# Scores of two attention branches: the keys' low parts in both halves of the partitions, and a second product over all 128 rows

## The chip, the cores and the metric

The kernel runs on one core of one Trainium2 chip. The metric is the device time of one launch in microseconds (us), the median of three runs. A difference below about 0.2% of it cannot be told from no change for this kernel: its three runs lie between 1477.23 and 1478.5 us.

## The reference, cut to what matters

Two layers of a hybrid block work on 256 latent tokens and 256 context tokens of width 1024. Each layer normalizes the tokens, projects them, and runs three attention branches side by side: grouped-query attention (8 query heads that share 2 key heads, 64 features a head), neighbourhood attention (8 heads of 64 features, with a bias for each position in the window), and latent attention (8 heads of 96 features). The branches are gated and merged, and a squared-ReLU MLP follows. The part that the change touches is the score of a query against a key, in the first two branches:

```
sc = jnp.einsum('bqkgd,btkd->bkgqt', qblk, k).astype(jnp.float32) * scale
p = jax.nn.softmax(sc, axis=-1).astype(v.dtype)
```

The context's queries are needed in the first layer alone, so there a head has two blocks of 128 latent queries against 512 keys and two blocks of 128 context queries against 256 keys; in the second layer it has the two latent blocks alone.

## The kernel before, in words

**Products.** TensorE (PE) takes float32r operands, which carry fewer bits than float32. So every operand is split in a high part (rounded) and a low part (what is left), and a product is made of three: high by high, high by low, low by high. The helper `mm3` (lines 762 to 764) issues these three for nearly all of the kernel. ScalarE (ACT) makes the high parts, VectorE (DVE) the low parts; for weights these are lines 699 and 700, one pair of instructions for a tile of 128x1024.

**Scores.** A head of 64 features fills only half of the 128 partitions that PE sums over. The neighbourhood and grouped-query branches use this: `stack_q` puts a head's high query parts on its own 64 partitions and its low parts on the other 64, and `stack_k` puts the head's high key parts in both halves. So one product over 128 rows (line 1518) makes high by high and low by high at once. A second product (line 1519) adds query-high by key-low. It reads only the head's own 64 partitions (rows 0 to 63 or 64 to 127), because there the key's low parts lie, in half of a slot. The latent branch has 96 features and uses `mm3` over 96 rows.

**One attention job** is a block of 128 queries of one head: scores on PE, the row's maximum on DVE (line 1654, or 1641 to 1645 with the bias), the exponential on ACT (1661), the scaling by the reciprocal sum on DVE (1672) or ACT (1670), four transposes on PE (1690 or 1694), the split of the transposed probabilities on ACT and DVE (808, 809). When the jobs of a head are done, PE multiplies with the values (1724, 1725). Three buffers hold the jobs under way. The branches run in the order neighbourhood, latent, grouped-query.

**What sets the order.** Every piece of work is a thread that asks for engines, buffers and events. A planner with a rough clock (fixed costs for each instruction, 0.43 us for a pair of score products) decides at build time which waiting instruction is issued next on each engine; on the chip each engine then runs its list in that order. Attention comes first where it can run, and dense items (projections, gates, output products) fill the rest. The dense items stand in a list (`SEQ`): `q k v` with a number are the neighbourhood branch's projections, `a0 a1 a2` those of the grouped-query branch, `g` gates. Of the grouped-query items, `a0` and `a1` wait until `a2` has got its slots (`gaslots`).

**Memory.** Everything but the weights lives in 41 slots of 4 KB a partition, which are lent in the order of the dense items (`needs`); a HALF or HALF_R is half a slot, a WHOLE a slot. Split weights have three tile pairs of their own (`wh0`, `wh1`, `wh2` with `wl0` to `wl2`); parts of the list add pairs out of slots for a while, but where the second layer's attention begins there are just the three. A weight tile takes a free pair as soon as it has arrived, and gives it back after its product.

Of the kernel before, what the change touches and what calls it, by code (L numbers as in the profile page):

```python
# [10 lines left out]
F32 = mybir.dt.float32  # L11
# [20 lines left out]
# attention units (pairs of heads) run in this order of branches, and so do their projections  # L32
# [11 lines left out]
# offsets in the packed column constants  # L44
# [8 lines left out]
RAW = 3          # weight tiles as they come from DRAM  # L53
SPLIT = 3        # weight tiles split in two parts
SLOTS = 41       # 4 KB slots (a partition) for everything else


# ---------------------------------------------------------------------------
# The schedule: the dense items in order, with the weight tiles that each one
# reads; shared by the host's packing and the program.  Words:  # L60
#   c0-7 first scale and shift by chunks; w 128 features of a later part of the modulation;
#   crow: room for the conditioning vectors as rows, until drop;
#   q k v + number: neighbourhood attention's projections; ckv rope l0-3: latent attention's;
#   a2 a0 a1 at: grouped-query attention's; yN yL yG: room for a branch's attention output
#   sN ...: that output split; gN0-7 oN0-3 ...: a branch's gates and products; W: output projection; M: MLP
# ---------------------------------------------------------------------------
# [16 lines left out]
def mix(items, extra, every=1):  # L83
    """`extra` spread among `items`, one after every `every` of those that read weights."""
    out, n, extra = [], 0, list(extra)
    for i in items:
        out.append(i)
        if i[2]:
            n += 1
            if extra and n % every == 0:  # L90
                out.append(extra.pop(0))
    assert not extra, len(extra)
    return out


def halves_of(l):
    """The token ranges that the sums before a norm are made in, latents first."""
    return [0, 1] if l == 0 else [0]


def word(l, w, wms):
    """The items of one word of SEQ."""
# [62 lines left out]
MLP_W = 48       # chunks of the modulation taken beside the first layer's MLP  # L165
# [92 lines left out]
WINDOW = (12, 8, 17)     # at the start, beside attention, otherwise  # L258
# [11 lines left out]
# ---------------------------------------------------------------------------  # L270
# The order of the instructions.  Every piece of the work is a thread (a
# generator) that asks for engines, buffers and events.  A rough clock of the
# engines decides which of the waiting instructions is issued next.
# ---------------------------------------------------------------------------
# [10 lines left out]
class Lender:  # L285
    """Lends a set of things; the lowest order is served first."""
# [24 lines left out]
class Arena(Lender):  # L311
    """Slots of [P, 2, T] words: WHOLE is a float32r slot (WHOLE_F float32), HALF and HALF_R are
    halves of a float32 or float32r one."""
# [43 lines left out]
class Banks(Lender):  # L357
    """PSUM banks, with a limit for each kind of use."""
# [19 lines left out]
class Window(Lender):  # L378
    """How many items may be under way."""
# [14 lines left out]
class Planner:  # L394
# [78 lines left out]
    def post(self, th, cmd):  # L473
        """Queues an instruction; ("any", ((engine, cost, fn), ...), slack) goes to the first that is free."""
# [10 lines left out]
    def dispatch(self):  # L485
        for e, p in self.pend.items():
            p[:] = [w for w in p if not w[4]]
            if p and self.busy[e] <= self.now + 1e-9:
# [4 lines left out]
                # TensorE runs at half its clock until it has been busy for a while  # L493
# [16 lines left out]
def a_(n):  # L510
    """Rough time of a ScalarE instruction over n columns."""
    return 0.07 + n * 0.00085
# [6 lines left out]
def v2_(n):  # L519
    return 0.07 + n * 0.00065  # L520


class Leaf:
    """Buffers that are given back after the last of n uses."""
# [10 lines left out]
class Opnd:  # L535
    """A (hi, lo) operand and the events that it waits for."""
# [8 lines left out]
class Prog:  # L545
# [22 lines left out]
    def fork(self, gen, pri=None):  # L568
        """A thread of its own, at the order of the item that is being built."""
        self.spawn(gen, self.cur[0], self.cur[1] if pri is None else pri)  # L570
# [39 lines left out]
    def needs(self, name, args):  # L610
        """The slots that an item owns; they are lent in the order of the items."""
# [4 lines left out]
        if name == "nak":  # L616
            return [WHOLE, HALF_R]
# [10 lines left out]
        if name == "gatr":  # L628
            return [pair] * 4 + [WHOLE, HALF_R]
# [30 lines left out]
    def take(self, mem, kind=WHOLE):  # L660
        """One of an item's own slots."""
# [5 lines left out]
    def take_pair(self, mem, n):  # L667
        """A slot for a (hi, lo) pair of n columns."""
# [15 lines left out]
    def transfer(self, n):  # L684
        """A transfer of n columns from when its descriptors are out."""
# [20 lines left out]
    def weights(self, keys, uses=1):  # L706
        """The split tiles of an item, given back after `uses` items have read them."""
# [15 lines left out]
    def it_raw(self, n, mem):  # L723
        """n more buffers for weights from DRAM, until it_less."""
# [15 lines left out]
    def it_more(self, n, mem):  # L740
        """n more buffers for split weights, until it_less."""
# [24 lines left out]
    def acc(self, out, a, b):  # L766
        """out = sum over k of a[k]^T b[k]; operands are (hi, lo) or Opnd."""
# [18 lines left out]
    def wcols(tl, n, w, c0=0, cw=None, off=0):  # L786
        """[(hi, lo)] of n row chunks in a split tile of row width w, columns c0:c0+cw."""
# [3 lines left out]
    def hcols(self, h, j):  # L791
        """h with features on partitions; j: 0 latents, 1 context, None both, by events of their own."""
# [11 lines left out]
    def hilo(self, hi, lo, src, n, scale=None, slack=0.0):  # L804
        """hi = round(src*scale), lo = src*scale - hi (both float32r)."""
# [15 lines left out]
    def it_wmc(self, l, c, mem):  # L821
        """Chunk c of the first scale and shift: both are wanted before anything else can start."""
# [37 lines left out]
    def it_crow(self, mem):  # L860
        """The two conditioning vectors along the columns of every partition, until it_drop."""
# [28 lines left out]
    def it_wm(self, l, part, fc, mem):  # L890
        """128 features of one of the modulation's six parts, as dot products along the columns."""
# [5 lines left out]
        # in the last layer the context is only normalized  # L897
# [33 lines left out]
    def stat(self, st, c, x, n, pos):  # L931
        """Adds the squares of chunk c to the sums of range st; the last chunk stays by itself."""
# [21 lines left out]
    def rstd(self, st, n, pos):  # L954
        """1/rms with tokens on partitions, one column for each 128 tokens."""
        nc = self.nc
        # the table of Sqrt is brought in before it is waited for
# [20 lines left out]
    def rstd_rows(self, st, n, pos):  # L978
        """1/rms of every token, on every partition (a PSUM bank)."""
# [14 lines left out]
    def norm_buffers(self, mem, key):  # L994
        """Sums of squares and three temporaries."""
# [33 lines left out]
    def norm_half(self, l, sc, sh, h, j):  # L1029
# [25 lines left out]
        if sc == SC1 and j == 1:  # L1055
            # the context's last use
# [4 lines left out]
    def it_start(self, mem):  # L1061
# [6 lines left out]
        # the conditioning vectors padded to 32 columns, and room for products of theirs  # L1068
# [62 lines left out]
    def project(self, keys, n, after):  # L1131
        """One weight tile, n tokens; `after(bank)` takes the product from its bank."""
# [1033 lines left out]
```

## Time and profile before

| | |
|---|---|
| median of three runs | 1477.95 us |
| lowest, highest | 1477.23, 1478.5 us |
| span of the profiled execution | 1471.1 us |
| busy share of the span: PE, DVE, ACT | 98%, 73%, 51% |
| chain that ended last: share of PE | 97% |
| score products: line 1518, line 1519 | 96, 96 |

The profiled execution is one run of its own; its span counts from the first to the last instruction. The median of the runs lies 6.85 us above it. In the profile, a group's row gives line, engine, operation, the tiles written and read, their shapes and count, then busy time and the mean ns of one, then the idle time of the engine before them. A matmul's duration there includes the time to run through the array, so the cost of one in a stream is read from start to start in the timeline. PEld is the load of the weights (the stationary operand), which can overlap a running matmul.

### The profile page before, as it was taken

What the parts mean: (1) busy time and instruction counts of PE and PEld (TensorE: products, weight loads), DVE (VectorE), ACT (ScalarE), POOL (GpSimd) and SP (SyncE); (2) the same over time, 40 slices, a digit from 0 to 9 for tenths busy, and PEclk for the clock granted to TensorE, in tenths of its full rate; (3) what the DMA queues carried; (4) which work ended last, traced back from release to release, by engine and by line L of the source; (5) the groups of instructions that cost most, each with busy time, mean ns of one, the idle gap of its engine ahead of it and who ended that gap; (6) DMA issues with size and microseconds to landing.
All of it is one profiled execution on the core that took longest, in us unless ns stands there. A gap on an engine that the chain in (4) does not pass through costs nothing.

```text
span 1471.1 us, 23933 instructions
## 1 busy us (share of the span) xinstructions
PE 1445.9 (98%) x9294; PEld 1287.8 (88%) x9294; DVE 1080.2 (73%) x2231; ACT 748.1 (51%) x1359; POOL 34.8 (2%) x74
## 2 busy tenths in 40 slices
PE   5999999999999999999999999999999999999997
PEld 3898789987778899988888889998899899999997
DVE  5537786867876998889867546767889887766665
ACT  4437776646772243423223234526778774645543
POOL 0000110000000000000000000000011000000000
PEclk9999999999999999999999999999999999999999
DMA  8511342252224553355655534335256336455551
GB/s 315 175 62 55 91 112 80 81 177 72 76 86 153 176 183 130 130 187 185 207 193 189 169 101 158 116 113 169 80 163 161 126 101 230 144 191 182 185 185 45
DMA packets 61778, 210.90 MB, mean 143 GB/s; under 512 B 7392, under 2 KB 9440, under 8 KB 61664
## 3 DMA queue, kind: packets, MB, share of 16 engines
q1 hardware_dynamic: 56448, 197.94, 41.0%
q0 software_dynamic: 4352, 10.49, 3.1%
q8 instruction: 73, 1.20, 0.3%
q10 hardware_dynamic: 864, 0.93, 0.2%
q14 instruction: 41, 0.34, 0.1%
HBM read 200.95 MB, written 1.05 MB: 137 GB/s over the span
## 4 chain that ended last, share of the span: by engine, by line
PE 97%; DMA 1%; DVE 1%; issue 0%; ACT 0%; SPq 0%; ACTq 0%
PE b L762 28%; PE b L763 28%; PE b L764 28%; PE b L1690 3%; PE b L1519 3%; PE b L1724 2%; PE b L1725 2%; PE b L1518 2%; PE b L1694 1%; DMA raw<-in_wts_dram 0%; PE b L835 0%; PE b L969 0%; PE b L986 0%; DMA s<-in_wts_dram 0%; PE b L1492 0%; DVE s L1089 0%
## 5 line engine op out<-in xcount | busy, mean ns | idle before, releaser
L762 PE MATMUL b<-s,wh 128*128 128x256 f32 (+1 forms) x1712 | 583.3, 341 | 0.0
L763 PE MATMUL b<-s,wh 128*128 128x256 f32 (+1 forms) x1712 | 573.0, 335 | 0.0
L764 PE MATMUL b<-s,wl 128*128 128x256 f32 (+1 forms) x1712 | 572.6, 334 | 0.0
L699 ACT CAST wh<-raw 128x1024 fp32r<-128x1024 f32 (+1 forms) x199 | 205.4, 1034 | 344.9 <-PE b L763 290.0
L762 PEld LDWEIGHTS b<-s,wh 128*128 128x128 f32 x1712 | 325.2, 190 | 38.9 <-issue 9.0
L764 PEld LDWEIGHTS b<-s,wl 128*128 128x128 f32 x1712 | 325.2, 190 | 32.9
L763 PEld LDWEIGHTS b<-s,wh 128*128 128x128 f32 x1712 | 325.6, 190 | 29.0
L700 DVE TENSOR_TENSOR wl<-raw,wh 128x1024 fp32r<-128x1024 f32 (+1 forms) x199 | 239.0, 1202 | 133.3 <-ACT wh L699 132.4
L905 DVE CUSTOM_DVE_ANT_0 s<-raw,s 128x512 f32<-128x512 f32 x236 | 162.5, 689 | 12.5 <-DMA raw<-in_wts_dram 8.0
L762 PE MATMUL b<-s,s 128*128 128x256 f32 (+4 forms) x512 | 152.3, 298 | 1.1 <-ACT s L1047 1.1
L763 PE MATMUL b<-s,s 128*128 128x256 f32 (+4 forms) x512 | 151.3, 295 | 0.2 <-DVE s L1048 0.2
L764 PE MATMUL b<-s,s 128*128 128x256 f32 (+4 forms) x512 | 150.8, 295 | 0.0
L809 DVE TENSOR_TENSOR s<-b,s 128x512 fp32r<-128x512 f32 (+3 forms) x151 | 101.2, 674 | 15.6 <-ACT s L808 14.7
L762 PE MATMUL b<-wh,s 128*128 128x256 f32 x368 | 108.2, 294 | 0.0
L1854 DVE SCALAR_TENSOR_TENSOR s<-b,mod,s 128x256 f32<-128x256 f32 x120 | 55.3, 481 | 66.5 <-PE b L764 66.2
L764 PE MATMUL b<-wh,s 128*128 128x256 f32 x368 | 104.0, 283 | 0.0
L763 PE MATMUL b<-wl,s 128*128 128x256 f32 x368 | 104.0, 283 | 0.0
L808 ACT CAST s<-b 128x512 fp32r<-128x512 f32 (+2 forms) x151 | 86.2, 578 | 33.6 <-PE b L764 12.8
L762 PEld LDWEIGHTS b<-s,s 128*128 128x128 f32 (+1 forms) x512 | 98.2, 192 | 2.4 <-ACT s L1047 1.3
L764 PEld LDWEIGHTS b<-s,s 128*128 128x128 f32 (+1 forms) x512 | 98.2, 192 | 2.0
L763 PEld LDWEIGHTS b<-s,s 128*128 128x128 f32 (+1 forms) x512 | 98.3, 192 | 1.4 <-DVE s L1048 0.5
L762 PEld LDWEIGHTS b<-wh,s 128*128 128x128 f32 x368 | 70.2, 191 | 4.5 <-issue 3.2
(156 smaller groups left out, 1856.1 us busy)
## 6 DMA issues: line engine op xcount, KB each, us to landing
raw<-in_wts_dram SPq DMA_DIRECT2D x301, 512.0 KB, 3.7
s<-in_wts_dram SPq DMA_DIRECT2D x59, 512.0 KB, 4.3
s<-in_xT_dram SPq DMA_DIRECT2D x16, 256.0 KB, 3.9
s<-s POOLq DMA_DIRECT2D x28, 128.0 KB, 4.0
s<-in_bias_dram POOLq DMA_DIRECT2D x16, 192.0 KB, 2.6
s<-s POOLq DMA_DIRECT2D x12, 256.0 KB, 3.2
raw<-in_wts_dram SPq DMA_DIRECT2D x4, 432.0 KB, 4.0
raw<-in_wts_dram SPq DMA_DIRECT2D x4, 384.0 KB, 3.5
```

Source lines behind the costliest of these rows:

```text
L699: yield from self.act(n, lambda: nc.scalar.copy(hi[:, :n], r[0][:, :n]), SL_W)
L700: yield from self.dve(n, lambda: nc.vector.tensor_tensor(lo[:, :n], r[0][:, :n], hi[:, :n].bitcast(F32), ALU.subtract), SL_W)
L762: mm(out, a[0], b[0], start=start, stop=False)
L763: mm(out, a[0], b[1], start=False, stop=False)
L764: mm(out, a[1], b[0], start=False, stop=stop)
L808: yield from self.act(n, lambda: nc.scalar.copy(hi, src), slack)
L809: yield from self.dve(n, lambda: nc.vector.tensor_tensor(lo, src, hi.bitcast(F32), ALU.subtract), slack)
L905: yield from self.dve(512, lambda: nc.vector.tensor_tensor_reduce(self.junk, w[0][:, r], self.crow[j][:, r], 1.0, 0.0, ALU.mult, ALU.add, ...
L1518: mm(out, q[:, i], k[s][:, j], start=True, stop=False)
L1519: mm(out, q[r, i], kl[r, j], start=False, stop=True)
L1690: nc.tensor.transpose(ps[:, c * P:(c + 1) * P], pt[:, c * P:(c + 1) * P], self.ident)
L1854: yield from self.dve(NLAT, lambda: nc.vector.scalar_tensor_tensor(o, bank.ap[:, i * NLAT:(i + 1) * NLAT], g[:, c, j:j + 1], x, ALU.mult, ...
```

## The change

`stack_k` now takes a whole slot for the low parts of the keys instead of half a slot, and writes the low parts of each head on that head's own 64 partitions, a column range for each head. A new step, `twice`, copies them to the other 64 partitions (two copies of 64x512, on DVE or ACT, whichever the planner finds free). The second score product then reads all 128 rows of the queries, high and low, so it adds query-high by key-low and query-low by key-low; the second of these was left out before. The room that the items ask for grows accordingly: half a slot more for each of the four `k` items and for `at`, in each layer. The diff also removes comments, which is left out here.

```
         if name == "nak":
-            return [WHOLE, HALF_R]
+            return [WHOLE] * 2
...
         if name == "gatr":
-            return [pair] * 4 + [WHOLE, HALF_R]
+            return [pair] * 4 + [WHOLE] * 2
...
     def stack_k(self, key, bank, mem):
-        slot, low = self.take(mem), self.take(mem, HALF_R)
+        slot, low = self.take(mem), self.take(mem)
         k, kl = slot.ap, low.ap
...
         def lo():
             for s in range(2):
-                nc.vector.tensor_tensor(kl[ROWS[s]], bank.ap[ROWS[s], :], k[ROWS[s], s, :].bitcast(F32), ALU.subtract)
+                nc.vector.tensor_tensor(kl[ROWS[s], s, :], bank.ap[ROWS[s], :], k[ROWS[s], s, :].bitcast(F32),
+                                        ALU.subtract)
+
+        def twice(act):
+            for s in range(2):
+                (nc.scalar.copy if act else nc.vector.tensor_copy)(kl[ROWS[1 - s], s, :], kl[ROWS[s], s, :].bitcast(F32))
         yield ("act", 4 * a_(T), hi, SL_E)
         yield ("dve", 2 * v_(T), lo, SL_E)
         self.unbank(bank)
-        self.qk[key], self.stacked[key] = [slot, low], ([k[:, s, :] for s in range(2)], kl)
+        yield ("any", (("dve", 2 * v2_(T), lambda: twice(False)), ("act", 2 * a_(T), lambda: twice(True))), SL_E)
+        self.qk[key], self.stacked[key] = [slot, low], tuple([x[:, s, :] for s in range(2)] for x in (k, kl))
...
     def scores(self, l, br, p, s):
-        q, (k, kl), r = self.stacked[kq][s], self.stacked[kk], ROWS[s]
+        q, (k, kl) = self.stacked[kq][s], self.stacked[kk]
         def make(out, i, j):
             mm(out, q[:, i], k[s][:, j], start=True, stop=False)
-            mm(out, q[r, i], kl[r, j], start=False, stop=True)
+            mm(out, q[:, i], kl[s][:, j], start=False, stop=True)
```

The new copies and the larger slots change what the planner does, so the change also moves instructions. The program's lines from 1191 on lie six further down (line 1519 becomes 1525). Of the twenty new copies (five key stacks in each layer, two copies each) eighteen stand on ScalarE and two on VectorE. In the first layer the order on TensorE keeps its shape. Where the second layer's attention begins it does not, at two places.

The first place is the end of the projection `k1` of the second layer on TensorE (`b` are PSUM banks, `s` slots, `wh` and `wl` the high and low parts of a weight tile). Before:

```order
L762 MATMUL b0_75<-s_303_6921,wh1_71 128x512
L763 MATMUL b0_75<-s_303_6921,wh1_71 128x512
L764 MATMUL b0_75<-s_303_6921,wl1_72 128x512
L762 MATMUL b3_78<-wh2_73,s_296_6753 128x256
L763 MATMUL b3_78<-wl2_74,s_296_6753 128x256
L764 MATMUL b3_78<-wh2_73,s_296_6753 128x256
```

And now:

```order
L762 MATMUL b2_77<-s_304_6932,wh2_73 128x512
L763 MATMUL b2_77<-s_304_6932,wh2_73 128x512
L764 MATMUL b2_77<-s_304_6932,wl2_74 128x512
L762 MATMUL b3_78<-s_297_6764,wh2_73 128x512
L763 MATMUL b3_78<-s_297_6764,wh2_73 128x512
L764 MATMUL b3_78<-s_297_6764,wl2_74 128x512
```

Before, the item `a0` (16 groups of three products of 256 columns, weights in other tiles) stood between `k1` and `k0`. Now `k0` follows `k1` at once and reads its weights from the same tile pair `wh2`, and so do `k3` and `q3` after it; `a0`, which waits for the slots of `a2`, holds the other two pairs and comes after the ninth job's scores.

The second place is TensorE between the scores of the fourth to the seventh job of the second layer (`ident` rows are the transposes of a job's probabilities). Before, from a transpose on:

```order
L1690 MATMUL b7_82<-ident_86,s_323_7698 128x128 x4
L762 MATMUL b3_78<-wh1_71,s_297_6754 128x256
L763 MATMUL b3_78<-wl1_72,s_297_6754 128x256
L764 MATMUL b3_78<-wh1_71,s_297_6754 128x256
L1518 MATMUL b6_81<-s_334_7857,s_316_7180 128x512
L1519 MATMUL b6_81<-s_335_7935,s_316_7180 128x512
L762 MATMUL b3_78<-wh1_71,s_298_6755 128x256
L763 MATMUL b3_78<-wl1_72,s_298_6755 128x256
```

And now:

```order
L1696 MATMUL b3_78<-ident_86,s_348_8139 128x128 x4
L1696 MATMUL b5_80<-ident_86,s_349_8189 128x128 x4
L1524 MATMUL b7_82<-s_336_7946,s_317_7191 128x512
L1525 MATMUL b7_82<-s_337_7947,s_317_7191 128x512
L1524 MATMUL b6_81<-s_336_7946,s_317_7191 128x512
L1525 MATMUL b6_81<-s_337_7947,s_317_7191 128x512
L762 MATMUL b2_77<-s_304_6932,wh2_73 128x256
```

Dense products stood between the jobs before; now scores and transposes follow each other. Between the third and the ninth job's scores there are 8 groups of three dense products where there were 29. From the first job's scores to the last job's transposes of this branch there are 42 where there were 59.

## The prediction

> **What bounds the kernel now.** I read the page first, then the chain of waits, then the timeline of TensorE around one score, then the busy times of the engines in the score stages. The page:
>
> ```profile
> span 1471.1 us, 23933 instructions
> PE 1445.9 (98%) x9294; PEld 1287.8 (88%) x9294; DVE 1080.2 (73%) x2231; ACT 748.1 (51%) x1359; POOL 34.8 (2%) x74
> ...
> PE 97%; DMA 1%; DVE 1%; issue 0%; ACT 0%; SPq 0%; ACTq 0%
> ...
> L762 PE MATMUL b<-s,wh 128*128 128x256 f32 (+1 forms) x1712 | 583.3, 341 | 0.0
> ```
>
> PE is the chain (97%), and its largest group has no idle time before it (0.0). So time taken from PE comes off the end, as long as PE does not begin to wait. But a busy PE is not a PE at its peak, so I look at starts. A latent score of the neighbourhood branch, PE's timeline (start us, us, engine, line):
>
> ```profile
> 109.14 0.39 PE L764 MATMUL b<-s,wl 128*128 128x512 f32 x1
> 109.37 0.28 PE L762 MATMUL b<-wh,s 128*128 128x256 f32 x1
> 109.48 0.28 PE L763 MATMUL b<-wl,s 128*128 128x256 f32 x1
> ...
> 109.72 0.39 PE L1518 MATMUL b<-s,s 128*128 128x512 f32 x1
> 110.05 0.50 PE L1519 MATMUL b<-s,s 64*128 64x512 f32 x1
> 110.48 0.39 PE L762 MATMUL b<-wh,s 128*128 128x256 f32 x1
> 110.70 0.28 PE L763 MATMUL b<-wl,s 128*128 128x256 f32 x1
> ```
>
> In a stream, a 512-column product takes 0.23 us from start to start (109.14 to 109.37) and a 256-column one 0.12 (109.48 follows 109.37 by 0.11; rounded). From the start of line 1518 to the start of line 763 there are two of 512 and one of 256, so 0.57 us would do; it takes 110.70 - 109.72 = 0.98. The pair costs **0.41 us** too much, in three pieces: 0.10 before the 64-row product, 0.20 after it, 0.10 after the next one. The weight loads tell why:
>
> ```profile
> 110.04 0.18 PEld L1519 LDWEIGHTS b<-s,s 64*128 64x128 f32 x1 [0.25 <-issue]
> 110.47 0.19 PEld L762 LDWEIGHTS b<-wh,s 128*128 128x128 f32 x1 [0.25 <-issue]
> ```
>
> Both loads, into the 64-row form and back out of it, stand idle first and begin with their own matmul (0.01 us ahead of it), where a load otherwise begins one matmul ahead. No engine is waited for ("issue"). PE empties itself when the row count changes. The same for 256 columns, where two pairs follow each other (context queries):
>
> ```profile
> 115.54 0.28 PE L1518 MATMUL b<-s,s 128*128 128x256 f32 x1
> 115.75 0.38 PE L1519 MATMUL b<-s,s 64*128 64x256 f32 x1
> ...
> 116.68 0.38 PE L762 MATMUL b<-wh,s 128*128 128x256 f32 x1
> 116.90 0.28 PE L763 MATMUL b<-wl,s 128*128 128x256 f32 x1
> ```
>
> Five products of 256 columns take 116.90 - 115.54 = 1.36 us instead of 0.60: 0.76 for two pairs, **0.38** each.
>
> **The change part by part.** *The second product over 128 rows.* How many there are, and what a row count that is not 128 costs elsewhere (line 1519 by itself, and the latent branch's three products over 96 rows, mean ns of one):
>
> ```profile
> L1519 PE MATMUL b<-s,s x88: 379/492/502, 107.3 to 1194.5; 64*128 64x512 f32 x56, 64*128 64x256 f32 x32
> L1519 PE MATMUL b<-s x8: 491/492/502, 1049.3 to 1160.4; 64*128 64x512 f32 x8
> ...
> L763 PE MATMUL b<-s,s 96*128 96x512 f32 x32 | 12.7, 396 | 0.0
> L764 PE MATMUL b<-s,s 96*128 96x512 f32 x32 | 12.5, 391 | 0.0
> ```
>
> 56 + 8 = 64 pairs of 512 columns at 0.41 us give 26.2 us, 32 of 256 columns at 0.38 give 12.2: **38.4 us** are spent on the changes of form. After the change every score product has 128 rows like its neighbours. The columns streamed stay the same, so its own time falls to 0.23 or 0.12 us. The latent branch already does just this (the same weights used twice in a row, then others) and its products take 391 and 396 ns, as long as line 764's dense one above (0.39). I take the full 38.4 us as gone from PE's own time.
>
> *The copies.* Twenty copies of 64x512, eighteen of them on ACT. The nearest row is the copy of the high parts:
>
> ```profile
> L1183 ACT CAST s<-b 64x512 fp32r<-64x512 f32 x40 | 23.2, 581 | 6.3 <-PE b L1492 3.8 <-PE b L764 2.0
> ```
>
> 18 x 0.58 = 10.4 us on an engine that is 51% busy, and each key stack is ready two copies, 1.2 us, later. They are off PE's chain where dense work covers them, so I price them at nothing except in the stages below; uncovered they would cost at most 10 stacks x 1.2 = 12 us.
>
> *Whether PE begins to wait.* Four stretches hold nearly all the pairs. Busy us of PE, PEld, DVE, ACT, POOL (counts in brackets), then clock and DMA, in the same order as the pairs below them:
>
> ```profile
> 115.00:190.00 75.00, 75.00 (x424) 59.26 (x422) 58.15 (x160) 54.78 (x129) 7.98 (x16) 1.00 0.28 79
> 355.00:430.00 75.00, 75.00 (x390) 56.94 (x390) 60.89 (x132) 54.99 (x129) 0.00 (x0) 1.00 0.22 75
> 1018.00:1066.00 48.00, 48.00 (x329) 40.65 (x329) 41.41 (x138) 38.51 (x83) 4.39 (x8) 1.00 0.30 95
> 1150.00:1195.00 45.00, 45.00 (x304) 37.18 (x302) 38.44 (x76) 37.32 (x81) 0.00 (x0) 1.00 0.29 95
> ...
> 115.00:190.00 75.00, 12.07 (x28) 5.12 (x28) 1.00 0.28 79
> 355.00:430.00 75.00, 13.74 (x32) 5.66 (x31) 1.00 0.22 75
> 1018.00:1066.00 48.00, 6.91 (x14) 2.56 (x14) 1.00 0.30 95
> 1150.00:1195.00 45.00, 7.92 (x16) 2.92 (x16) 1.00 0.29 95
> ```
>
> With 28, 32, 14 and 16 pairs at 0.4 us the first, second and fourth stretch shrink to about 63.8, 62.2 and 38.6 us, and DVE's work is then 91%, 98% and 100% of them (ACT's, with one more stack's copies, 88%, 90% and 100%). So DVE takes PE's place where it is full: nothing in the first stretch, and I put 2 us each on the second and the fourth. Their ends are 0 (the engines pack fully) and, if DVE reaches 90% of a stretch, 60.9/0.9 - 62.2 = 5 and 38.4/0.9 - 38.6 = 4 us.
>
> The third stretch, the neighbourhood branch of the second layer, is another matter, since there the order changes (the two places shown with the change). *First*, `k0`, `k3` and `q3` now use the same weight tile pair as the item ahead of them, so each must be split after that one has ended. What a split costs from the release on is to be seen before, where the next item did not wait for it (ACT, DVE, PE):
>
> ```profile
> 1000.32 1.05 ACT L699 CAST wh<-raw 128x1024 fp32r<-128x1024 f32 x1 [2.13 <-PE b L763]
> 1001.41 1.23 DVE L700 TENSOR_TENSOR wl<-raw,wh 128x1024 fp32r<-128x1024 f32 x1 [1.06 <-ACT wh L699]
> 1000.35 0.28 PE L762 MATMUL b<-wh,s 128*128 128x256 f32 x1
> 1006.10 0.40 PE L762 MATMUL b<-s,wh 128*128 128x512 f32 x1
> ```
>
> `k1` ended at 1000.3, the split was done at 1001.41 + 1.23 = 1002.64, and PE ran `a0` from 1000.35 to 1006.10 meanwhile. Now `a0` is gone from there, and PE waits 2.3 us for `k0` and again for `k3`: **4.6 us**. (`q3` stands among jobs and is counted with them. What ends this wait is ACT and then DVE; everything on PE is queued behind it.)
>
> *Second*, the jobs have less dense work between them. This is the count of dense groups in the third stretch:
>
> ```profile
> L762 PE MATMUL b<-wh,s 128*128 128x256 f32 x33 | 11.1, 335 | 0.0
> L762 PE MATMUL b<-s,wh 128*128 128x256 f32 x24 | 7.4, 309 | 0.0
> ```
>
> 57 groups of three at 3 x 0.12 = 0.36 us; now 17 fewer, so 6.1 us of PE's work move behind this stretch. PE's work in it becomes 48 - 14 x 0.41 - 6.1 = 36.2 us, while DVE's 41.4 stays. PE must wait for it, at least 41.4 - 36.2 = 5.2 us, and at most 48 - 36.2 = 11.8 if DVE stays as loose as it is now. I take **7**, nearer the lower end, since DVE's looseness now is waiting for PE.
>
> The moved dense work is not lost: it stands later, where PE has nothing to wait for. But what PE waits is lost, because PE is the chain. The sum: 38.4 - 4.6 - 7 - 2 - 2 = **22.8 us** gained. The profiled span of 1471.1 us becomes about 1448, and with the 6.85 us by which the median of the runs lies above this span, 1477.95 becomes **1455 us**. By the ends of the terms the gain is 38.4 - 9.8 = 28.6 to 38.4 - 4.6 - 11.8 - 9 = 13, so 1449 to 1465.
>
> **The rivals.** (a) *PE hardly waits.* For it: PE has no idle time in any of these stretches now, and dense work could be read ahead of. Against: the order shows `k0` on a tile pair that is not free. Gain about 36 to 38 us, 1440 to 1442. (b) *DVE and ACT bind everywhere:* all stage terms at or past their upper ends, and every new copy uncovered. Gain 5 to 13 us, 1465 to 1473. Against: in the latent stage PE keeps pace without a change of form, by a chain without waits. (c) *Slower: room.* Five more half slots a layer starve the dense items, so that weight tiles are used one at a time through the whole second layer's attention. Each such tile costs 2.3 us; beside the 11 us of stage waits it takes 27.4 / 2.3 = 12 more tiles in single file to eat the gain. The order shows three in a row. About 1480. (d) *The change does not do what it says:* the second load, on the rows of the matmul that is running, cannot be hidden, and 0.18 us of load stays open in each of 96 pairs, 17 us: 1472. Against: line 763's matmuls at 0.11 us distance have their loads hidden on the same 128 rows.
>
> The Trainium skill, TensorE: Matmul & The Clock Gate, section "Part 3: Packing small matmuls — row/col tiling", says that a weight load overlaps running matmuls only where its row group differs, which would make (d) the rule for a pair of two 128-row products. The trace disagrees, in the start distances of 0.11 and 0.23 us above on equal rows. The same skill's page TensorEngine Tiling (Array Packing), section "Key Properties", says that a change of the tiling mode drains TensorE; by that, the two gaps of 0.25 us before the loads are the drain.
>
> **How the numbers follow.** The forecast (1449 to 1465) has 0.60, (a) 0.18, (b) 0.13, (c) 0.03, (d) 0.06. The likeliest is 1455 us. The range of 8 in 10 runs from 1441 to 1466: the forecast's own, and most of (a). For this kernel 0.2%, about 3 us, is what can be told from no change. Faster by more: 0.95, within it: 0.02, slower: 0.03.
>
> **What would show it.** Lines 1524 and 1525 at 0.23 us (0.12 for 256 columns) from start to start, with no idle time before their weight loads: right on the changes of form; a gap of 0.2 us left: (d). Two gaps of about 2.3 us on PE ahead of `k0` and `k3` of the second layer, ended by line 700 on DVE, and 5 to 12 us of PE idle among the first jobs behind them: right on the order. No such gaps: (a). Idle time on PE spread over all four stages, ended by DVE's lines 809 and 1654: (b). The prediction is wrong if PE's idle time before the second layer's latent branch is under 5 us or over 20.

## The result and the profile after

The changed kernel takes 1458.27 us (median of four runs, 1457.82 to 1459.33) beside 1477.59 for the kernel before on the same chip (1477.12 to 1478.5): **a ratio of 0.9872, 95% interval 0.9858 to 0.9886**. It is 19.3 us faster. The prediction said 1455 and a gain of 22.8.

The page of the changed kernel, its span, its busy times, its chain and its largest group of products:

```profile
span 1457.6 us, 23967 instructions
PE 1419.6 (97%) x9294; PEld 1290.2 (89%) x9294; DVE 1076.7 (74%) x2236; ACT 752.9 (52%) x1374; POOL 34.8 (2%) x74
...
PE 89%; DVE 5%; DMA 3%; ACT 2%; issue 1%; POOL 0%; ACTq 0%; SPq 0%; DVEq 0%; POOLq 0%
...
L762 PE MATMUL b<-s,wh 128*128 128x256 f32 (+1 forms) x1704 | 579.4, 340 | 3.1 <-ACT wh L699 1.9
```

PE's share of the chain falls from 97% to 89%, and its largest group, which had no idle time ahead of it, now has 3.1 us. So PE has begun to wait. First the products themselves, PE's timeline around a pair of 512 columns and around two pairs of 256 (start us, us, engine, line):

```profile
110.23 0.40 PE L1524 MATMUL b<-s,s 128*128 128x512 f32 x1
110.47 0.40 PE L1525 MATMUL b<-s,s 128*128 128x512 f32 x1
110.70 0.28 PE L762 MATMUL b<-wh,s 128*128 128x256 f32 x1
110.82 0.27 PE L763 MATMUL b<-wl,s 128*128 128x256 f32 x1
...
115.28 0.28 PE L1524 MATMUL b<-s,s 128*128 128x256 f32 x1
115.40 0.28 PE L1525 MATMUL b<-s,s 128*128 128x256 f32 x1
115.52 0.28 PE L1524 MATMUL b<-s,s 128*128 128x256 f32 x1
115.64 0.28 PE L1525 MATMUL b<-s,s 128*128 128x256 f32 x1
115.76 0.28 PE L762 MATMUL b<-wh,s 128*128 128x256 f32 x1
115.88 0.28 PE L763 MATMUL b<-wl,s 128*128 128x256 f32 x1
```

From line 1524 to line 763 the first takes 0.59 us, where it took 0.98 before. Five products of 256 columns take 0.60 instead of 1.36. The pieces that the form change cost are gone entirely. The weight loads show why (the same view of the load queue):

```profile
110.23 0.19 PEld L1525 LDWEIGHTS b<-s,s 128*128 128x128 f32 x1
110.47 0.19 PEld L762 LDWEIGHTS b<-wh,s 128*128 128x128 f32 x1
```

No idle time is shown ahead of them, and each begins one product ahead of its own. Now the waits of PE. These are all of its products between 970 and 1112 us that waited more than 0.25 us; the bracket gives the wait and what ended it:

```profile
979.98 0.50 PE L762 MATMUL b<-s,wh 128*128 128x512 f32 x1 [0.95 <-ACT wh L699]
981.25 0.50 PE L764 MATMUL b<-s,wl 128*128 128x512 f32 x1 [0.53 <-DVE wl L700]
987.48 0.50 PE L762 MATMUL b<-s,wh 128*128 128x512 f32 x1 [0.95 <-ACT wh L699]
988.74 0.50 PE L764 MATMUL b<-s,wl 128*128 128x512 f32 x1 [0.53 <-DVE wl L700]
...
995.80 0.65 PE L1696 MATMUL b<-ident,s 128*128 128x128 f32 x4 [0.43 <-DVE s L1678]
997.86 0.38 PE L764 MATMUL b<-s,wl 128*128 128x256 f32 x1 [0.72 <-DVE wl L700]
1006.92 0.58 PE L1730 MATMUL b<-s,s 128*128 128x256 f32 x1 [2.27 <-ACT s L808]
1008.18 0.58 PE L1731 MATMUL b<-s,s 128*128 128x256 f32 x1 [0.67 <-DVE s L809]
1028.79 0.39 PE L1731 MATMUL b<-s,s 128*128 128x256 f32 x1 [0.76 <-DVE s L809]
...
1075.20 0.47 PE L762 MATMUL b<-s,s 96*128 96x512 f32 x1 [1.56 <-DMA s<-s]
1103.96 0.47 PE L762 MATMUL b<-s,s 96*128 96x512 f32 x1 [0.72 <-DMA s<-s]
1110.31 0.66 PE L1696 MATMUL b<-ident,s 128*128 128x128 f32 x4 [1.53 <-ACT s L1676]
```

The first four are `k0` and `k3` of the second layer, 1.48 us of idle time each. The next five stand among the first jobs of its neighbourhood branch, 4.85 us in all; one of them, 0.72 us, waits for the low part of a weight tile (line 700). The last three are its latent branch, 3.81 us, and two of them end with a transfer from slot to slot (`s<-s`, rows of the keys). How much that is in all, against before, shows in the busy times of the engines over this stretch of 180 us (PE, PEld, DVE, ACT, POOL, then mean granted clock, DMA share, GB/s). Before:

```profile
960.00:1140.00 180.00, 180.00 (x1278) 164.80 (x1277) 139.99 (x349) 120.11 (x233) 15.97 (x30) 1.00 0.48 136
```

After, with the grouped-query stages of the two layers as second and third row:

```profile
960.00:1140.00 180.00, 168.16 (x1183) 155.67 (x1182) 133.11 (x327) 124.20 (x240) 16.02 (x30) 0.98 0.45 131
...
345.00:425.00 80.00, 79.56 (x463) 68.30 (x462) 75.47 (x162) 63.25 (x145) 0.00 (x0) 1.00 0.27 93
1140.00:1184.00 44.00, 43.81 (x340) 41.64 (x339) 40.73 (x81) 40.05 (x87) 0.00 (x0) 1.00 0.32 106
```

PE was never idle there before; now it is for 180 - 168.16 = **11.8 us**, and part of the rest runs at a lower clock, which takes at most 3.4 us more (last section). The grouped-query stages lose only 0.44 and 0.19 us. So the 38.4 us are gone from the products, and 38.4 - 19.3 = 19.1 of them are lost again. Of these, 11.8 us are idle time in one part of the second layer. Idle time is less than what a wait costs: the two waits of `k0` are 1.48 us of idle time and cost 2.0 us from start to start (shown further down). The 19.1 us have not been added up wait by wait.

### The profile page after: what moved, and what is told of

The parts are those of the page before. It is cut to its first block, busy times and chain, and to the rows that moved or that the text cites. A ratio compares the mean times of both kernels' runs of the same rounds, so it can differ in the third digit from the quotient of the medians.

```text
span 1457.6 us, 23967 instructions
## 1 busy us (share of the span) xinstructions
PE 1419.6 (97%) x9294; PEld 1290.2 (89%) x9294; DVE 1076.7 (74%) x2236; ACT 752.9 (52%) x1374; POOL 34.8 (2%) x74
## 4 chain that ended last, share of the span: by engine, by line
PE 89%; DVE 5%; DMA 3%; ACT 2%; issue 1%; POOL 0%; ACTq 0%; SPq 0%; DVEq 0%; POOLq 0%
PE b L762 26%; PE b L763 26%; PE b L764 26%; PE b L1696 2%; PE b L1731 2%; DMA s<-s 2%; PE b L1730 2%; DVE wl L700 1%; PE b L1524 1%; PE b L1525 1%; ACT s L1667 1%; DVE s L809 1%; DMA raw<-in_wts_dram 1%; PE b L1700 1%; PE b L835 1%
## 5 line engine op out<-in xcount | busy, mean ns | idle before, releaser
L762 PE MATMUL b<-s,s 128*128 128x256 f32 (+4 forms) x520 | 154.3, 297 | 2.3 <-DMA s<-s 2.3
L763 PE MATMUL b<-s,s 128*128 128x256 f32 (+4 forms) x520 | 153.0, 294 | 0.0
L764 PE MATMUL b<-s,s 128*128 128x256 f32 (+4 forms) x520 | 152.9, 294 | 0.0
L762 PEld LDWEIGHTS b<-s,s 128*128 128x128 f32 (+1 forms) x520 | 99.4, 191 | 3.8 <-issue 1.7
L764 PEld LDWEIGHTS b<-s,s 128*128 128x128 f32 (+1 forms) x520 | 99.4, 191 | 2.0
L763 PEld LDWEIGHTS b<-s,s 128*128 128x128 f32 (+1 forms) x520 | 99.5, 191 | 1.1
L808 ACT CAST s<-b 128x512 fp32r<-128x512 f32 (+3 forms) x151 | 85.4, 578 | 28.2 <-PE b L764 11.8
L699 ACT CAST wh<-s 128x1024 fp32r<-128x1024 f32 x35 | 36.7, 1049 | 72.6 <-PE b L763 64.4
```

The lines of the kernel that those rows point to most:

```text
L699: yield from self.act(n, lambda: nc.scalar.copy(hi[:, :n], r[0][:, :n]), SL_W)
L762: mm(out, a[0], b[0], start=start, stop=False)
L763: mm(out, a[0], b[1], start=False, stop=False)
L764: mm(out, a[1], b[0], start=False, stop=stop)
L808: yield from self.act(n, lambda: nc.scalar.copy(hi, src), slack)
```

## The experiments

Theory A, from the prediction: PE itself pays each change of form, and the loss against the full 38.4 us comes from the new order of the work in the second layer, which the larger slots bring. Against it stood B (DVE and ACT bind in the score stages as soon as PE is faster, in whichever order), the copies as the cause (their own time, and key stacks that are ready later), and, for what stands between the two orders, C (weight tiles in single file are the whole loss) and D (PE only reaches the same jobs earlier and waits there).

### The 128-row product alone

```
-            mm(out, q[r, i], kl[r, j], start=False, stop=True)
+            mm(out, q[:, i], kl[:, j], start=False, stop=True)
```

> The kernel before, but the second score product reads all 128 rows of the low tile as it is: no copies, no larger slots, every engine's order as before. (The lower 64 rows then add query-low of a head by key-low of the other head of its pair, a term of the size of the one that was left out before.) Theory A (PE pays each change of form itself, and the changed kernel's loss of 19 us against the full 38.4 comes from the new order that the larger slots bring): 1477.6 - 38.4 = 1439 us, PE idle in the second layer's neighbourhood stage 0 to 3 us. Theory B (VectorE and ScalarE bind in the score stages as soon as PE is faster, in whichever order): about the changed kernel's time, 1452 to 1460, with PE idle 10 us or more in the four score stages.

Measured: **1439.14 us** (1438.6 to 1440.73), the kernel before beside it 1476.53 (1473.61 to 1479.36), ratio 0.9749 (0.9729 to 0.9768). The same stretch of its profile:

```profile
960.00:1140.00 180.00, 179.99 (x1320) 170.26 (x1319) 148.95 (x347) 138.01 (x271) 15.91 (x30) 1.00 0.49 141
```

PE is practically never idle. DVE does more in these 180 us than before (148.95 to 139.99) or after the change (133.11), and still does not hold PE up. B falls: with the old order the other engines keep pace with the faster PE. In medians 37.4 of the 38.4 us come off the end. It is also the fastest kernel of this study, 19 us below the changed one. Run once more on another chip, beside three kernels below:

> The kernel with the 128-row product on the shared low tile alone, once more, for the comparison on one chip: 1437 to 1441 us, that is 17 to 21 us less than the changed kernel beside it.

Measured: 1439.29 us (1437.19 to 1440.6), the kernel before 1474.35, ratio 0.9757 (0.9743 to 0.9772). Here 35.1 us come off the end, and it is 17.0 us less than the changed kernel beside it.

### The changed kernel's order with the old product

```
-            mm(out, q[:, i], kl[s][:, j], start=False, stop=True)
+            mm(out, q[r, i], kl[s][r, j], start=False, stop=True)
```

> The changed kernel with its larger slots, its copies and its order on every engine, but the second score product on 64 rows as before. Theory A: the order alone costs time, and the changes of form come back: 1458.3 + 38.4 = 1497 less what the slower PE hides of the 9 us of waits among the jobs, so 1486 to 1497, slower than before. Theory B: the order costs nothing as long as PE is slow enough, so 1476 to 1479.

Measured: **1489.3 us** (1487.36 to 1491.4), ratio 1.0087 (1.0068 to 1.0105): slower than before, as A said. Together with the first experiment this gives all four corners (medians):

| | second product on 64 rows | on 128 rows |
|---|---|---|
| order of the kernel before | 1476.5 | 1439.1 |
| order of the changed kernel | 1489.3 | 1458.3 |

The order costs 12.8 us even with the slow PE, and 19.1 with the fast one; the rows save 37.4 us in the old order and 31.0 in the new one. In the stretch from 960 to 1140 us PE is idle for 180 - 171.28 = 8.72 us in the new order with the slow product, and for 11.84 with the fast one. So 3.1 of the extra 6 us are longer waits; the rest is not accounted for. (The lower right corner is from the chip of the result, the others share one chip. On the chip where both kernels with 128 rows ran, the order costs 17.0 us.)

### Larger slots without copies

```
-            return [WHOLE, HALF_R]
+            return [WHOLE] * 2
...
-        slot, low = self.take(mem), self.take(mem, HALF_R)
-        k, kl = slot.ap, low.ap
+        slot, low = self.take(mem), self.take(mem)
+        k, kl = slot.ap, low.ap[:, 0, :]
...
-            mm(out, q[r, i], kl[r, j], start=False, stop=True)
+            mm(out, q[:, i], kl[:, j], start=False, stop=True)
```

(`at`'s slots grow in the same way.)

> Larger slots and the 128-row product on the shared low tile, no copies: k0, k3 (and here also q3) of the second layer follow each other on one weight tile pair, as in the changed kernel. Theory A with the room as cause: 1453 to 1460, as the changed kernel, with the waits ahead of k0 and k3 still there. If the copies (key stacks ready 1.2 us later, 10.4 us more on ScalarE) are the cause: 1438 to 1443.

Measured: **1456.12 us** (1453.3 to 1459.58), ratio 0.9863 (0.9841 to 0.9885). That is 17.0 us above the 128-row product alone on the same chip, as much as the changed kernel lies above it on another. So the larger slots alone bring a loss of that size; no copy is needed for it.

### The copies alone, with and without the planner's knowledge

Three kernels take the copies apart. In the first, the planner counts them and they run, added to the kernel with the 128-row product alone and in its slots (each copy writes the low parts onto themselves; eighteen of the twenty stand on ScalarE and two on VectorE):

```
+        def again(act):
+            for s in range(2):
+                (nc.scalar.copy if act else nc.vector.tensor_copy)(kl[ROWS[s]], kl[ROWS[s]].bitcast(F32))
+        yield ("any", (("dve", 2 * v2_(T), lambda: again(False)), ("act", 2 * a_(T), lambda: again(True))), SL_E)
```

> Slots as before, the 128-row product on the shared low tile, and two added copies for each key stack, of the low parts onto themselves (20 copies of 64x512, all on ScalarE), so the stacks are ready 1.2 us later and ScalarE has 11 us more work, without the larger slots. Theory A (the copies are hidden beside PE): within 3 us of the kernel with the 128-row product alone, 1437 to 1443. If the copies are what costs: 1448 to 1458.

Measured: **1449.92 us** (1446.82 to 1452.0), ratio 0.9829 (0.9812 to 0.9846), 10.6 us above the kernel without them beside it (1439.29). By what was expected of it the copies are what costs, and A's hidden copies look wrong. But the planner had moved the work here too. So in the second kernel it still counts the copies, and they are not run:

```
         def again(act):
-            for s in range(2):
-                (nc.scalar.copy if act else nc.vector.tensor_copy)(kl[ROWS[s]], kl[ROWS[s]].bitcast(F32))
+            pass
```

> The order of the kernel with planned copies and slots as before, without the copies themselves. If the planner's new order is what cost 10.6 us there: 1445 to 1452. If the copies' own time did: 1437 to 1442. Both in part: between.

Measured: **1448.24 us** (1445.41 to 1448.96), ratio 0.9813 (0.9796 to 0.983). Most of the 10.6 us is there without a single copy: 9.0 by the medians, which are from two chips, 8.3 by the ratios, and 6.7 against the next kernel (1441.58), which ran on the same chip in the old order. The stretch of both kernels, the copies run in the first and not in the second:

```profile
960.00:1140.00 180.00, 175.43 (x1275) 164.99 (x1274) 144.37 (x342) 134.60 (x256) 15.92 (x30) 1.00 0.47 142
```

```profile
960.00:1140.00 180.00, 175.42 (x1266) 165.11 (x1264) 143.52 (x340) 127.69 (x244) 15.98 (x30) 0.99 0.48 141
```

PE is idle for 4.57 and 4.58 us: the same. ACT has 6.9 us less to do in the second, and these waits do not change. In the third kernel the copies run, and the planner does not know of them, so the order is that of the kernel with the rows alone:

```
+            for s in range(2):
+                nc.scalar.copy(kl[ROWS[s]], kl[ROWS[s]].bitcast(F32))
```

> The order of the kernel with the 128-row product alone on every engine, and twenty copies of the low parts onto themselves added on ScalarE right behind each stack's high parts, which the planner does not know of. If copies are hidden beside PE as long as the order is the old one: 1437 to 1443. If their own time costs, by ScalarE's instructions behind them: 1447 to 1455, the 10 us of the kernel with planned copies.

Measured: **1441.58 us** (1440.67 to 1446.29), ratio 0.9778 (0.9757 to 0.98), PE idle for 180 - 179.13 = 0.87 us in the stretch:

```profile
960.00:1140.00 180.00, 179.13 (x1310) 169.03 (x1309) 148.22 (x346) 142.86 (x278) 15.97 (x30) 1.00 0.48 141
```

The copies' own time is worth some 2 to 3 us (2.3 by the medians, 3.1 by the ratios, both on different chips), and as the intervals of the two ratios overlap, it cannot be told from nothing. The same test on the changed kernel, with its order on every engine and no copies:

```
         def lo():
             for s in range(2):
-                nc.vector.tensor_tensor(kl[ROWS[s], s, :], bank.ap[ROWS[s], :], k[ROWS[s], s, :].bitcast(F32),
+                nc.vector.tensor_tensor(kl[ROWS[s], 0, :], bank.ap[ROWS[s], :], k[ROWS[s], s, :].bitcast(F32),
                                         ALU.subtract)
         def twice(act):
-            for s in range(2):
-                (nc.scalar.copy if act else nc.vector.tensor_copy)(kl[ROWS[1 - s], s, :], kl[ROWS[s], s, :].bitcast(F32))
+            pass
...
-            mm(out, q[:, i], kl[s][:, j], start=False, stop=True)
+            mm(out, q[:, i], kl[0][:, j], start=False, stop=True)
```

> The changed kernel's order on every engine, word for word, but the twenty copies are left out of the program (the planner still counts them); the 128-row product reads the shared low tile. If the order is what costs (larger slots and planned copies): 1452 to 1459, as the changed kernel. If the copies' own time costs (the stacks late, ScalarE busier): 1439 to 1446.

Measured: **1458.89 us** (1455.41 to 1460.39), ratio 0.9892 (0.9875 to 0.991), as slow as the changed kernel with its copies. So the loss is the order, whether larger slots or planned copies bring it about. The two losses do not add: the larger slots alone already bring 17.0 us.

### The changed kernel again, and with its weight tiles in turn

Is the single file of weight tiles ahead of `k0` and `k3` a loss of its own? The changed kernel was run again, beside one in which `a0` stands behind `a2` in the list of the second layer; the four projections then use the three tile pairs in turn.

```
-    "... k1 w w a0 k0 w yN w k3 w q3 attn a2 w gL0 ..."
+    "... k1 w w k0 w yN w k3 w q3 attn a2 a0 w gL0 ..."
```

> The changed kernel once more, unchanged, for the comparison on one chip: 1455 to 1461 us. A stretch of about 6.8 us at half the granted clock is expected behind the wait of 2.27 us in the second layer's neighbourhood stage; where a run has no such wait or a shorter one, none.

> The changed kernel with a0 behind a2 in the second layer's list, so that k1, k0, k3 and q3 use the three weight tile pairs in turn; the jobs still have few dense groups between them (six score products' blocks in a row stand without any). Theory A (two separate losses): the two waits ahead of k0 and k3, 3.6 us by the changed kernel's trace, are gone, the waits among the jobs stay or grow, so 2 to 5 us less than the changed kernel run beside it. Theory C (the weight tiles in single file are the whole loss): 15 us or more less, near 1440. Theory D (PE only reaches the same jobs earlier and waits there instead): within 2 us of the changed kernel.

Measured: the changed kernel **1456.24 us** (1452.08 to 1457.86, ratio 0.9869, 0.9846 to 0.9891); with `a0` later **1457.47** (1455.71 to 1459.65, ratio 0.9883, 0.9866 to 0.9899). No gain. PE's waits in the second one, all above 0.2 us between 970 and 1112 us:

```profile
998.85 1.54 PE L1696 MATMUL b<-ident,s 128*128 128x128 f32 x6 [4.45 <-ACT s L1676]
1004.92 0.38 PE L1731 MATMUL b<-s,s 128*128 128x256 f32 x1 [0.98 <-DVE s L809]
1009.44 0.39 PE L1731 MATMUL b<-s,s 128*128 128x256 f32 x1 [1.50 <-DVE s L809]
1012.90 0.66 PE L1696 MATMUL b<-ident,s 128*128 128x128 f32 x4 [1.42 <-ACT s L1676]
1102.16 0.76 PE L762 MATMUL b<-s,s 96*128 96x512 f32 x1 [2.06 <-DMA s<-s]
```

The waits ahead of `k0` and `k3` are gone, and the first jobs make PE wait 8.35 us, where it was 4.85 in the first profile of the changed kernel. Over the stretch of 180 us PE is idle for 10.61 us in the changed kernel's run beside it and for 10.55 here. D holds: PE reaches the first job's transposes earlier and waits there for its softmax. A's sum of two separate losses, and C, fall. What PE has to do meanwhile are dense groups of three products; between the third and the ninth job's scores there are 29 in the order of before, 8 in the changed kernel, 2 here. The waits grow as these go away. That this number is the cause is argued from the three, not shown: the order with planned copies has 32 and still 1.1 us of wait there.

### Both products on 64 rows

```
-            mm(out, q[:, i], k[s][:, j], start=True, stop=False)
+            mm(out, q[r, i], k[s][r, j], start=True, stop=False)
```

> The kernel before with both score products on 64 rows (query-low by key-high is left out), so that the pair is of one form and stands among 128-row products. The order is as before and the number of changes of form is the same (one into 64 rows, one out of it, for a pair, or fewer where two pairs follow each other). If the change of form is what costs: 1468 to 1479, a pair 0.41 us or less over its stream time. If each 64-row product costs something by itself (the trace shows 0.10 us ahead of one and 0.30 after it): 0.3 to 0.4 us more for each of 96, 1506 to 1516.

Measured: **1460.46 us** (1459.69 to 1465.0), ratio 0.9898 (0.9876 to 0.9919), 16.1 us faster than before, below the range that was expected of a cost by change of form, and far from that of a cost by product. The timeline shows where the count of changes was wrong:

```profile
114.69 0.28 PE L764 MATMUL b<-wh,s 128*128 128x256 f32 x1
114.90 0.38 PE L1518 MATMUL b<-s,s 64*128 64x256 f32 x1
115.12 0.28 PE L1519 MATMUL b<-s,s 64*128 64x256 f32 x1
115.24 0.28 PE L1518 MATMUL b<-s,s 64*128 64x256 f32 x1
115.36 0.28 PE L1519 MATMUL b<-s,s 64*128 64x256 f32 x1
115.56 0.39 PE L762 MATMUL b<-wh,s 128*128 128x256 f32 x1
115.79 0.28 PE L763 MATMUL b<-wl,s 128*128 128x256 f32 x1
```

Six products of 256 columns from line 764 to line 763 would stream in 0.72 us and take 115.79 - 114.69 = 1.10. So one excursion into 64 rows costs 0.38 us, whether one product or four stand in it; inside it they follow each other at 0.12. The 192 products of 64 rows lie in 67 unbroken rows where before there were 96, one for each pair: 29 fewer at 0.4 us make 11.6 us. The profiled spans differ by 1471.1 - 1458.3 = 12.8, and the interval of the ratio reaches down to 0.0081 x 1476.5 = 12 us. The rest is not accounted for.

The Trainium skill, TensorEngine Tiling (Array Packing), section "Key Properties", says that changing the tiling mode, not just the tile, drains TensorE. The trace agrees: 0.38 us for an excursion, and nothing between the 64-row products themselves. But not every row count does this, as the prediction's "PE empties itself when the row count changes" would have it. In the latent branch of the kernel before, a product over 96 rows starts 0.12 us behind one over 128 rows and 256 columns (1076.16 to 1076.28 us), and the next one 0.23 us later, as within a stream. Of these row counts, only 64 is shown to cost.

## Why the prediction was right, and where it was not

**The changes of form, 38.4 us: right.** The pairs in the timeline lost their 0.41 and 0.38 us, and with the order unchanged 37.4 us arrive at the end (35.1 on a second chip). The rival that the second load could not be hidden (d) is wrong. The rule on TensorE: Matmul & The Clock Gate, section "Part 3: Packing small matmuls — row/col tiling", in the Trainium skill, by which a load overlaps a running product only where the row group differs, does not hold here: line 1525's load starts at 110.23 with line 1524's product on the same 128 rows, and the next product follows at 0.24 us.

**The copies at nothing: right for their time, and wrong for what the planner makes of them.** Their own time is worth 2 to 3 us, if anything. But the step that priced them asked only what covers them on ACT. To a planner an instruction that it counts is also a reason to issue other things in another order, and that alone brought a ratio of 0.9813 where 0.9757 stood. The prediction took the new order as it was and did not ask which part of the change brings it; its rival (c) named the room alone.

**`k0` and `k3`, 4.6 us: the mechanism was right and the size nearly, the sum was not.** They wait for their weight tiles. The step took the time from the release to the end of both parts of the split, 2.3 us for each. To compare with that, the products at the start of `k0`, PE's timeline:

```profile
978.64 0.39 PE L764 MATMUL b<-s,wl 128*128 128x512 f32 x1
979.98 0.50 PE L762 MATMUL b<-s,wh 128*128 128x512 f32 x1 [0.95 <-ACT wh L699]
980.32 0.40 PE L763 MATMUL b<-s,wh 128*128 128x512 f32 x1
981.25 0.50 PE L764 MATMUL b<-s,wl 128*128 128x512 f32 x1 [0.53 <-DVE wl L700]
981.58 0.39 PE L762 MATMUL b<-s,wh 128*128 128x512 f32 x1
```

From 978.64 to 981.58 four products of 512 columns take 2.94 us where 4 x 0.23 = 0.92 would do, so `k0` costs 2.0 us, of which 0.95 + 0.53 = 1.48 are idle time. It is less than 2.3 because `mm3` reads the high part in its first two products: PE starts when ACT is done (line 699) and waits again, for line 700, only at the third product. But the term does not add to the next one: without these waits the first jobs waited 3.5 us longer, and the time did not fall.

**The neighbourhood stage, 7 us: the size is near, the reason holds in part.** Idle time of PE ahead of the latent branch is 2 x 1.48 + 4.85 = 7.8 us, within the 5 to 20 that the prediction named; the 7 us of this term stand against the 4.85. The step let DVE's total of 41.4 us bound the stage. That total is not the bound. From 990 to 1036 us, where these jobs run in the changed kernel, DVE is busy for 40.55 of 46 us; with the rows alone it is busy for 38.89 of 40 us (992 to 1032), and PE waits for nothing. But for a short time DVE and ACT are both nearly full: from 1000 to 1010 us, around the longest wait, they are busy for 9.63 and 9.80 of 10 us. The waits end with lines 808, 809 and 1678, the steps of a single job from its scores to its product with the values, and one with line 700. So a job's steps are late while PE has no dense work to cover them. How much of that is the job's own latency, and how much the work that stands ahead of it on ACT and DVE, the runs do not separate.

**The grouped-query stages, 2 + 2 us: too dear.** 0.44 and 0.19 us. DVE is busy for 75.47 of 80 us in the first, and PE hardly waits. The lower end of the two terms, that the engines pack fully, was the right one.

**Not in the sum:** the latent branch's waits, 3.81 us of idle time. The step said that the moved dense work "stands later, where PE has nothing to wait for", and that was wrong. Two of these waits end with the transfer of rotated key rows (line 1409, issued at 1070.20 and 1098.46 us), which is itself issued only when an earlier transfer from slot to slot has landed. The transfers of the second head's rows, 256 KB each (rows of transfers: KB each, median us from issue to landing), in the changed kernel and with the rows alone:

```profile
s<-s POOLq DMA_DIRECT2D x12, 256.0 KB, 4.2
```

```profile
s<-s POOLq DMA_DIRECT2D x12, 256.0 KB, 3.2
```

They land later in all of the orders that differ from the old one (3.8 to 4.2 us) and not in those that keep it (3.2 to 3.3). That this is why PE waits there is not shown. The prediction looked at the neighbourhood stage alone and took what stood behind it as it was. The lower clock was not in the sum either (below).

**From span to median.** The prediction added 6.85 us to the span of 1448. But in all of the runs for which both are given, the time is 1.7 to 2.0 us above the span. The profiled execution of the kernel before was then one of its shorter ones: its runs lie between 1472.91 and 1479.36 us over the four chips on which it ran. In spans the forecast of 1448 missed by 8 to 10 us (measured 1456.0 to 1457.6), and the offset made up for most of it. The loss was 38.4 - 19.3 = 19.1 us instead of 15.6. So the time came within 3.3 us by a mechanism that was right in its first term, and in the rest partly by luck: errors of both signs, and an offset that belonged to one execution.

**The rivals.** (a), that PE hardly waits, describes the product with the old order (1439), not this change. (b) is wrong. (c), slower by room, had the right place: larger slots bring an order with single file and fewer dense groups among the jobs. Its price, a fixed loss for each tile in single file, is wrong: with the tiles in turn nothing was gained. The whole order costs 12.8 us with the old product, as the second experiment shows, which the 38.4 us outweigh.

## What to carry to other kernels

Price a change by what it does to the instructions, and apart from that by what it does to their order: run the new instruction in the old order before adding what it seems to need, since here the order that the copies and the room for them bring cost half of what the product gained. In this kernel a product on 64 rows among products on 128 costs more than one on 128 rows that also multiplies low parts by low parts; if it must stay, put several of them side by side. Waits that are cleared one after the other do not add where the same latency stands behind both.

## What the runs showed of the hardware

A short wait can be followed by several microseconds at half of PE's clock, and is not always. In the profiled execution of the changed kernel, the granted clock falls to one half at the end of the wait of 2.27 us that begins at 1004.6; ten microseconds of it:

```profile
1004.00:1014.00 10.00, 7.05 (x30) 5.94 (x29) 9.04 (x41) 8.49 (x19) 1.07 (x2) 0.66 0.22 72
```

A mean of 0.66 over 10 us is 6.8 us at one half, so at most 3.4 us of work are lost (PE is idle for part of it). When the same kernel was run again, the same wait (2.28 us, ended by the same line) left the clock at 1.00, so what was expected of that run was wrong; there the low clock followed a wait of 1.72 us at 1099.3 instead (again the row of ten microseconds, and one of seven):

```profile
1004.00:1014.00 10.00, 6.33 (x46) 5.72 (x47) 9.61 (x44) 8.32 (x19) 1.06 (x2) 1.00 0.29 90
1099.00:1106.00 7.00, 5.28 (x24) 4.49 (x23) 6.46 (x15) 6.30 (x12) 2.65 (x5) 0.76 0.83 209
```

That second stretch is 7 x 0.24 x 2 = 3.4 us at one half, half the length of the first. The Trainium skill, TensorE: Matmul & The Clock Gate, section "Part 1: The HAM clock gate (the "warmup" mystery)", tells of free-running windows of about 3.4 us and of a return to half the clock after at least one idle window. The lengths agree, being one and two such windows; the condition does not, since neither of these two waits lasts a whole window. A longer wait, 4.45 us from 994.4 on in the kernel with `a0` later, does not bear the condition out either: a mean of 0.59 from 996 to 998 us puts the fall at 996.4, 2.0 us into the wait.
